# One-core hybrid attention block: value rows per head and partition, heads' outputs through DRAM, values one item behind, and a shorter start

## The chip, the core and the metric

One core of a Trainium2 chip runs the whole program. The metric is the device time of one execution in microseconds (us); the time before is the median of three runs. TensorE is called PE, VectorE DVE, ScalarE ACT, GpSimd POOL; SP issues most DMAs. "x" beside a row is a count, and a granted clock of 1.00 is PE's full clock.

## The reference, cut to what matters

A block on x of 1024 tokens by 1024 channels, in float32: an RMS norm, one wide projection, stick-breaking attention (8 heads of 64), an HGRN2 recurrence (4 heads of 128), a gated merge, and an MLP of width 4096.

```python
xn = rmsnorm(x, norm1_g[layer])
u = xn @ w_in[layer]
q_sb, k_sb, v_sb, f_raw, i_hg, q_hg, g_hg, gate_sb, gate_hg = split(u)
z = einsum('bhqd,bhkd->bhqk', qi, k) * scale
log_beta = log_sigmoid(z)
log_rem = where(mask, log_beta - z, 0)
between = cumsum(log_rem, axis=3, reverse=True) - log_rem
w = where(mask, exp(log_beta + between), 0)
o_sb = einsum('bhqk,bhkd->bhqd', w, v)
o_hg = hgrn2_chunkwise(silu(q_hg), k_hg, i_hg, log_f)   # then norm, * silu(g_hg)
merged = g_a * (o_sb @ w_o_sb) + g_b * (o_hg @ w_o_hg)
h = x + merged @ w_out
out = rmsnorm(h + square(relu(rmsnorm(h) @ w_ff1)) @ w_ff2)
```

## The kernel before

**Precision and product counts.** A float32 matrix is used as a high and a low part (a "split": ACT casts the high part at L154, DVE subtracts it at L159), so each product is three matmuls. `hi_lo_sent` makes the low part another way: ACT copies the negated value, and an accumulating DMA of POOL adds the source. Large products are done with seven instead of eight half-size products, which need sums of halves of the weights (`ValuePair`, blocks "11", "12", "21", "22") and of the normalised input (the forms of `early_form`, built from `early_whole`, which copies a high part and lets a POOL DMA add the low part).

**The start (0 to 186 us).** x is normalised and transposed in halves of 512 tokens (`norm_transpose`; its low parts xnl are DVE's, L346). In the gaps of that work the stream `front` runs the first head's q and k projection (`pjqk`) and the first two products of the values v and of HGRN's inputs i. `raw_units[0]` is the first block of attention's output gate: its product 1 (`pga`) and product 4 (`pgq`), which uses the weight wga0t, split from block 21 less a sum of other blocks. Finished values go to the DRAM table `vrows`, one row per token, 512 wide (8 heads x 64), behind a row of zeros.

**Attention (186 to 400 us).** 64 items (head h, block qb), in the order qb = 7, 0, 6, 1, 5, 2, 4, 3 within a head. An item's scores z (PE) give 1 - beta by a sigmoid (ACT, tile rm), a product scan on DVE (L1093) turns them into cumulated remainders, PE transposes these (`pw`), and ACT and DVE evict them as high and low weights wTh and wTl (L1141, L1147). Weights are used as differences, so V is the difference of neighbouring value rows: `v_load` reads the rows twice, once shifted by one, and `v_split` subtracts and splits them. Two items with neighbouring qb (7 and 6, 0 and 1, 5 and 4, 2 and 3) share a values product (`values`, tile po, numbered head_qc); it runs when the second item of the pair lies two items back. Scores run two items ahead and the scan one. Between them the loop takes steps of a fill stream (`st`): gate and HGRN projections `pga`, `pgq`, `pjf`, `pjq`. PE executes in order; main work and fill are two lanes, and a block of fill may not start before the main block two back.

A head's outputs ot have its own 64 rows twice, as a high and a low share; one half is written by an ACT DMA to rows of `osb` (SBUF, a pair of heads each), the other is added there by a POOL DMA.

**After attention (400 us on).** HGRN levels with raw jobs 5 to 7 of the gates as fill, the merge, and the MLP. Jobs 4 to 7 put `osb` 0 to 3 into the product with w_o_sb. In jobs 1 to 7, product 4 runs first and ACT copies it out of PSUM (p14); DVE adds the first half of product 1 to it.

Of the kernel before, what the change touches and what calls it, by code (L numbers as in the profile page):

```python
# [14 lines left out]
ALU = mybir.AluOpType  # L15
# [4 lines left out]
P = 128  # L20
# [19 lines left out]
def kernel(  # L40
# [34 lines left out]
    def slot(name, dt=F32):  # L75
        return spool.tile([P, 1024], dt, tag="s", name=name)
# [11 lines left out]
    def dram(name, shape):  # L88
        return scratch.tile(shape, F32, tag=name, name=name)
# [48 lines left out]
    def load(dst, src):  # L138
        last_load[0] = after(nc.sync.dma_start(dst, src), last_load[0])
# [38 lines left out]
    def halves():  # L178
        return ((i, slice(i * 512, (i + 1) * 512)) for i in range(2))
# [478 lines left out]

    qk, osb = {}, {}

    vrows = dram("vrows", [T + 1, SBW])
    vt, vraw = {}, {}

    def first_row():
        zero = half("vzero")[0:1, :]
        nc.gpsimd.memset(zero, 0.0)
        nc.gpsimd.dma_start(vrows[0:1, :], zero)

    def v_load(h):
        vraw[h] = slot(f"vr{h}")  # L670
        for i, cs in halves():
            load(
                vraw[h][:, cs].rearrange("p (t d) -> p t d", d=DHS),
                vrows[1 - i : T + 1 - i, h * DHS : (h + 1) * DHS].rearrange(
                    "(t p) d -> p t d", p=P
                ),
            )

    def v_split(h):
        r = vraw.pop(h)  # L680
# [61 lines left out]
    class ValuePair:  # L742
# [19 lines left out]
        def minus(self, out, x, y):  # L762
            for kp in range(2):
# [2 lines left out]
                    op=ALU.subtract,  # L766
                )

        WEIGHT = {1: "11", 2: "21", 3: "22", 4: "21", 5: "11", 6: "22", 7: "12"}

        def split(self, m):
# [39 lines left out]
        def p2(self, tb):  # L811
            v = half(f"v1{tb}")
            nc.scalar.copy(v, self.X[tb])
            Z = bank(f"viZ{tb}")
            yield from self.steps(2, {tb: Z}, True)
            nc.vector.tensor_tensor(out=v, in0=v, in1=Z, op=ALU.add)
            self.store(vrows, 1, 0, tb, v)

        def store(self, rows_, first, half_, tb, v):
            r0 = first + half_ * 512 + tb * P  # L820
            nc.gpsimd.dma_start(rows_[r0 : r0 + P, :], v)

        def x4(self):
            banks = {tb: bank(f"viP{tb}") for tb in range(4)}
# [13 lines left out]
        def x7(self):  # L838
            self.product(7, self.X, False)
            for tb in range(4):  # L840
                self.u3[tb] = half(f"vu3{tb}")
                nc.scalar.copy(self.u3[tb], self.X[tb])
                v = self.p4[tb]
                nc.vector.tensor_tensor(out=v, in0=v, in1=self.X[tb], op=ALU.add)
                self.store(vrows, 1, 1, tb, v)

        def y5(self):
            self.Y = {tb: bank(f"viY{tb}") for tb in range(4)}
            self.product(5, self.Y, True)
            for tb in range(4):  # L850
                v = self.u3[tb]
                self.last = add(v, v, self.Y[tb])
                self.store(irows, 0, 1, tb, v)

        def y3(self):
            self.product(3, self.Y, False)
            for tb in range(4):
                v = self.u2[tb]
                nc.vector.tensor_tensor(out=v, in0=v, in1=self.Y[tb], op=ALU.add)
                self.store(irows, 0, 0, tb, v)  # L860

    irows = dram("irows", [T, HGW])
    vi = ValuePair()
# [290 lines left out]
        return (h, qc) if seen[h, qc] == 2 else None  # L1154

    ots, sums = {}, deque()

    def values(h, qc):
        open_block("main")
        tiles = wTt.pop((h, qc))  # L1160
        nkb = 2 * qc + 2
        po = bank(f"po{h}_{qc}")[:, 0:256]
        for kb in range(nkb):
            for i in range(2):
                matmul(
                    po,
                    v_stat(h, kb),
                    tiles[kb // 4][i][:, kb % 4, :],
                    start=kb == 0 and i == 0,
                    stop=kb == nkb - 1 and i == 1,  # L1170
                )
        if qc in (3, 0) and h not in ots:
            ots[h] = [slot(f"ot{h}"), 0]
        ot = ots[h][0]
        nc.scalar.copy(ot[:, qc * 256 : (qc + 1) * 256], po)
        ots[h][1] += 1
        if ots[h][1] == 4:
            pair, r = h // 2, (h % 2) * DHS
            if pair not in osb:
                osb[pair] = slot(f"osb{pair}")  # L1180
            dst, other = osb[pair][r : r + DHS, :], ot[DHS - r : 2 * DHS - r, :]
            nc.scalar.dma_start(dst, ot[r : r + DHS, :])
            sums.append(lambda: nc.gpsimd.dma_start(dst, other, accum_op=ALU.add))

# [49 lines left out]
    def hg_job(h, key):  # L1234
        c0, ep = {
            "f": (C_F, f_epilogue), "q": (C_QH, lambda h: silu_epilogue(h, "q")),
            "g": (C_GH, lambda h: silu_epilogue(h, "g")),
        }[key]
        u = cols_unit(f"w{key}{h}", [(W_IN, c0 + h * P, P)])
        u.sent = h == 0  # L1240
        j_hg[h] = proj_jobs([(f"pj{key}{h}", u, ep(h))], xn)

    def hg_jobs(h):
# [328 lines left out]
    def raw_job(cb):  # L1572
        u = raw_units[cb]

        def steps_of(ps, wt, w0, half_, k0, start):
            wh, wl = u.hl[wt]
            for k in range(4):
                c = (w0 + k) * P
                xh, xl = xn.mov(k0 + k, half_)
                three(  # L1580
                    ps, wh[:, c : c + P], wl[:, c : c + P], xh, xl, start and k == 0, k == 3, True
                )
                if k % 2 == 1:
                    yield

        def body():
            p1, p14, g1 = (half(f"{n}_{cb}") for n in ("p1", "p14", "g1"))
            if cb >= 6:
                load_g1(cb - 6)
            if cb:  # L1590
                p4 = bank(f"pgq{cb}")
                yield from steps_of(p4, 1, 0, 1, 4, True)
                nc.scalar.copy(p14, p4)
            ps = bank(f"pga{cb}")
            yield from steps_of(ps, 0, 0, 0, 0, True)
            hi_behind[0] = nc.scalar.copy(p1, ps)
            nc.scalar.dma_start(pd[cb][:, 0, :], p1)
            if cb:
                st.prefetch()
            hi_behind[0] = None  # L1600
            if cb:
                add(p14, p1, p14)
            else:
                p4 = bank(f"pgq{cb}")
                yield from steps_of(p4, 1, 0, 1, 4, True)
                add(p14, p1, p4)
            nc.gpsimd.dma_start(pd[cb][:, 1, :], p14)
            yield from steps_of(ps, 0, 4, 0, 4, False)
            nc.scalar.activation(g1, ps, AF.Sigmoid, bias=gate_bias(0, cb))
            nc.scalar.dma_start(gd[cb], g1)  # L1610
            if cb >= 4:
                a_sb.put(cb - 4, osb[cb - 4])

        return st.add([u], body)

# [809 lines left out]
    norm1(range(4, NT))  # L2425
    front.advance(10, 1)
    raw_units[0].split()
    norm_transpose(xn, 1, 0, 4, None, lambda: front.advance(1, 1))
    turns["on"] = False
    for kp in range(2):  # L2430
        for b in ("12", "22"):
            vi.load(b, kp)
    turn_vectors(1, 6)
    lower_bounds()
    first_row()
    vi.minus("11", "12", "11")
    for half_, j in ((1, 0), (1, 1), (0, 0)):
        early_whole(half_, j)
    front.finish(j_first)
    raw_units[0].split_t()  # L2440
    vi.minus("12", "22", "12")
    vi.minus("22", "22", "11")
    vi.minus("21", "21", "22")
    vi.split(4)
    st.finish(j_raw[0])
    blocks = [qk_parts(h) for h in range(1, NHS)] + [(((C_GH, P),), g_store)]
    proj = [ProjPair(i, *blocks[2 * i : 2 * i + 2]) for i in range(4)]
    proj[0].load()
    early_op((1, 1), (1, 0), (1, 1), ALU.add)
    early_op((1, 0), (0, 0), (1, 0), ALU.subtract)  # L2450
    vi.x4()
    early_op((0, 0), (1, 1), (0, 0), ALU.subtract)
    early_form(6, *early_at((0, 0)))
    vi.split(6)
    early_form(7, *early_at((1, 0)))
# [58 lines left out]
    for i, it in enumerate(items):  # L2514
        if i + 1 < len(items):
            weights(*items[i + 1])
        if i + 2 < len(items):
            scores(*items[i + 2])
        if i % 2 == 1:
            next(wsums, None)  # L2520
        ahead = it[0] + 1
        if ahead < NHS and i % NHS in (1, 2, 6):
            {1: v_load, 2: qk_load, 6: v_split}[i % NHS](ahead)
        if sums and i % NHS == 4:
            sums.popleft()()
        want = n_first + (i + 1) * (n_fill - n_first) // len(items)
        st.advance(want - done, j_first_hg)
        done = want
        before = ready.popleft()[1] if ready and ready[0][0] < i - 1 else None

        def between():
            if before:
                values(*before)

        r = turn(*it, between)
        if i == len(items) - 2:
            attended[0] = turn_lo[0]
        if it[1] != NT - 1:
            between()
        if r:  # L2540
            ready.append((i, r))
# [141 lines left out]
```

## Time and profile before

| | |
|---|---|
| three runs | 1466.84, 1470.25, 1471.27 us |
| median | 1470.25 us |
| the profiled execution | 1469.17 us, span 1467.5 us |
| mean granted clock of PE | 0.994 |
| DMA moved over the span | 280.21 MB, mean 191 GB/s |

All durations come from the one profiled execution. Its span runs from the first to the last instruction; 1.7 us of its time lie around it. Busy PE at a clock below 1.00 is PE doing the same work longer, so idle time alone does not tell PE's whole loss.

### The profile page before, as it was taken

Reading aid. Unit: us, or ns where it says so; the run is one execution under the profiler, and the core shown is the slowest. Engines: PE = TensorE matmul, PEld = TensorE weight load, DVE = VectorE, ACT = ScalarE, POOL = GpSimd, SP = SyncE. Lnnn points to the kernel's source line nnn. Section 1 sums busy time; section 2 is a strip of 40 time slices with the busy share of each in tenths; the row PEclk is TensorE's granted clock in tenths of the full one; section 3 lists DMA queues with packets and bytes.
Section 4 is the critical chain, followed back from the end, with each engine's and each line's share of the span. In section 5 each row is a group of like instructions: output and inputs, shape, how many; then the busy total and the mean of one; then the engine's idle time right before and its main releaser. Section 6 shows DMA issues by size and latency. Waiting matters only on the chain. (4 is left out here: it accounts for less than half of the span.)

```text
span 1467.5 us, 19123 instructions
## 1 busy us (share of the span) xinstructions
PE 1422.1 (97%) x6990; PEld 1185.8 (81%) x6990; DVE 1069.0 (73%) x1486; ACT 683.3 (47%) x1115; POOL 183.0 (12%) x343
## 2 busy tenths in 40 slices
PE   8899999997999999999999999999999999999997
PEld 7678877786788888888887788888888888888886
DVE  6856568886976868668876898666776766768765
ACT  6553457665634434333334575444444533533433
POOL 3231222323100001101011110000000000000032
PEclk9999999999999999999999999999999999999999
DMA  9786699999512326855359623444444975676824
GB/s 307 167 279 186 194 256 235 216 214 204 118 58 65 101 65 206 289 170 174 130 184 300 212 93 129 158 158 158 158 158 158 348 267 201 232 277 244 281 104 181
DMA packets 187430, 280.21 MB, mean 191 GB/s; under 512 B 44444, under 2 KB 108488, under 8 KB 187336
## 3 DMA queue, kind: packets, MB, share of 16 engines
q1 hardware_dynamic: 163256, 207.41, 43.9%
q0 software_dynamic: 19696, 62.93, 15.5%
q10 hardware_dynamic: 4384, 8.65, 1.8%
q8 instruction: 55, 0.90, 0.3%
q14 instruction: 39, 0.32, 0.1%
HBM read 191.39 MB, written 83.36 MB: 187 GB/s over the span
## 5 line engine op out<-in xcount | busy, mean ns | idle before, releaser
L1093 DVE TENSOR_TENSOR_SCAN rm<-rm,bits 128x512 f32<-128x512 f32 (+6 forms) x72 | 87.5, 1223 | 23.9 <-ACT rm L1067 23.8
L154 ACT CAST whid<-w 128x1024 fp32r<-128x1024 f32 x30 | 31.6, 1053 | 153.3 <-PE pm L131 85.4
L131 PE MATMUL pm<-wlod,sh 128*128 128x512 f32 x240 | 93.5, 390 | 0.0
L131 PE MATMUL pm<-whid,sl 128*128 128x512 f32 x240 | 93.4, 389 | 0.0
L131 PE MATMUL pm<-whid,sh 128*128 128x512 f32 x240 | 93.4, 389 | 0.0
L131 PE MATMUL pm<-tl,sh 128*128 128x512 f32 (+1 forms) x210 | 81.3, 387 | 0.0
L131 PE MATMUL pm<-th,sl 128*128 128x512 f32 (+1 forms) x210 | 81.3, 387 | 0.0
L131 PE MATMUL pm<-th,sh 128*128 128x512 f32 (+1 forms) x210 | 81.3, 387 | 0.0
L159 DVE TENSOR_TENSOR wlod<-w,whid 128x1024 fp32r<-128x1024 f32 x30 | 36.7, 1223 | 56.2 <-ACT whid L154 56.1
L2239 POOL TENSOR_SCALAR fss<-fss 128x1 f32<-128x1 f32 x8 | 4.5, 562 | 562.5 <-ACT fsc L2234 561.9
L159 DVE TENSOR_TENSOR sl<-sa,sh 128x1024 fp32r<-128x1024 f32 x56 | 68.3, 1219 | 1.2 <-ACT sh L154 1.2
L1141 ACT ACTIVATE wTh<-pw,minus_one 128x128 fp32r<-128x128 f32 (+3 forms) x96 | 55.2, 597 | 29.3 <-PE pw L134 24.4
L154 ACT CAST sh<-sa 128x1024 fp32r<-128x1024 f32 x56 | 57.2, 1046 | 7.2 <-DMA sa<-ad 7.2
L1067 ACT ACTIVATE rm<-z 128x512 f32<-128x512 f32 (+3 forms) x96 | 44.4, 503 | 28.0 <-PE z L131 20.8
L1147 DVE SCALAR_TENSOR_TENSOR wTl<-pw,wTh 128x128 fp32r<-128x128 f32 (+3 forms) x96 | 49.7, 544 | 10.0 <-ACT wTh L1141 6.5
L131 PEld LDWEIGHTS pm<-wlod,sh 128*128 128x128 f32 x240 | 45.0, 188 | 9.8 <-DVE wlod L159 0.6
L131 PEld LDWEIGHTS pm<-whid,sh 128*128 128x128 f32 x240 | 45.1, 188 | 9.4
L131 PEld LDWEIGHTS pm<-whid,sl 128*128 128x128 f32 x240 | 45.0, 187 | 9.4
L134 PE MATMUL pw<-ident,rm 128*128 128x128 f32 x288 | 44.5, 279 | 6.8 <-DVE rm L1093 6.6
L131 PE MATMUL pX<-sql,t1h 128*128 128x512 f32 x128 | 50.0, 391 | 0.4 <-DVE sql L159 0.4
L131 PE MATMUL pX<-sqh,t1l 128*128 128x512 f32 x128 | 50.0, 390 | 0.1
L131 PE MATMUL pX<-sqh,t1h 128*128 128x512 f32 x128 | 49.8, 389 | 0.0
(986 smaller groups left out, 4451.9 us busy)
## 6 DMA issues: line engine op xcount, KB each, us to landing
w<-in_w_ff_dram SPq DMA_DIRECT2D x72, 512.0 KB, 4.8
sa<-ad SPq DMA_DIRECT2D x56, 512.0 KB, 6.7
ad<-a SPq DMA_DIRECT2D x32, 256.0 KB, 4.3
ad<-s SPq DMA_DIRECT2D x16, 512.0 KB, 3.8
tw<-in_w_out_dram POOLq DMA_DIRECT2D x24, 256.0 KB, 8.9
vi<-in_w_in_dram SPq DMA_DIRECT2D x10, 512.0 KB, 4.8
x<-in_x_dram SPq DMA_DIRECT2D x8, 512.0 KB, 7.6
qkh<-qkh POOLq DMA_DIRECT2D x16, 256.0 KB, 4.1
```

Source lines behind the costliest of these rows:

```text
L131: return pe(nc.tensor.matmul(*a, **k))
L134: return pe(nc.tensor.transpose(dst, src, ident))
L154: hi_last[0] = after(in_turn("act", nc.scalar.copy(dst, src)), hi_behind[0])
L159: nc.vector.tensor_tensor(out=dst, in0=src, in1=hi.bitcast(F32), op=ALU.subtract),
L1067: nc.scalar.activation(rm[:, s0 : s0 + m], z[:, :m], AF.Sigmoid, scale=-0.125)
L1093: sc = nc.vector.tensor_tensor_scan(out=rr, data0=rr, data1=bits[:, 1024 - nk + a : 1024 - nk + b][:, ::-1], initial=rm[:, b : b + 1] if i ...
L1141: nc.scalar.activation(th[:, 0:n, qs], src, AF.Identity, bias=minus_one),
L1147: nc.vector.scalar_tensor_tensor(out=tl[:, 0:n, qs], in0=src, scalar=-1.0, in1=th[:, 0:n, qs].bitcast(F32), op0=ALU.add, op1=ALU.subtract,),
L2239: nc.gpsimd.tensor_scalar(out=ssq, in0=ssq, scalar1=1.0 / D, scalar2=EPS, op0=ALU.mult, op1=ALU.add)
```

## The change

What it does, part by part:

1. `vrows` is laid out per head and partition: head h, partition p, then 64 values of each of the 8 token tiles, behind a tile that holds zero in its last partition. A store of v now writes pieces of 64 values; a load of a head's rows is 128x512, 127x512 and 1x512 in rows of 2 KB.
2. `v_split` of the next head moves from item 6 to item 5 of a head; `values` runs when its second item lies one item back.
3. `osb` in SBUF becomes a DRAM table `osd`, to which ACT's and POOL's DMAs write; raw jobs 5, 6 and 7 load it back (one pair, one pair, two pairs).
4. In jobs 5 to 7 product 4 runs after the first half of product 1 and is added straight from PSUM, as in job 0.
5. The first HGRN head's weights no longer use `hi_lo_sent`.
6. In the start, blocks "12" and "22" are loaded and "11" and "21" formed before the second half's transposes; wga0t follows these; "21" is made without the changed "22", as (21 - 22) + (12 - 11). `vi.split(4)` and one `early_op` move too.

```diff
-    vrows = dram("vrows", [T + 1, SBW])
+    vrows = dram("vrows", [NHS, P, (NT + 1) * DHS])
...
     def v_load(h):
-        vraw[h] = slot(f"vr{h}")
-        for i, cs in halves():
-            load(
-                vraw[h][:, cs].rearrange("p (t d) -> p t d", d=DHS),
-                vrows[1 - i : T + 1 - i, h * DHS : (h + 1) * DHS].rearrange(
-                    "(t p) d -> p t d", p=P
-                ),
-            )
+        r = vraw[h] = slot(f"vr{h}")
+        n = NT * DHS
+        load(r[:, :n], vrows[h, :, DHS:])
+        load(r[1:P, n:], vrows[h, 0 : P - 1, DHS:])
+        load(r[0:1, n:], vrows[h, P - 1 : P, :n])
...
+        def plus(self, out, x, y):
+            for kp in range(2):
+                add(self.raw[out, kp], self.raw[x, kp], self.raw[y, kp])
...
+            t = half_ * 4 + tb
+            if rows_ is vrows:
+                dst = rows_[:, :, (t + 1) * DHS : (t + 2) * DHS].rearrange("h p d -> p h d")
+                v = v.rearrange("p (h d) -> p h d", d=DHS)
...
+    osd = [dram(f"osd{pair}", [P, T]) for pair in range(NHS // 2)]
...
-            if pair not in osb:
-                osb[pair] = slot(f"osb{pair}")
-            dst, other = osb[pair][r : r + DHS, :], ot[DHS - r : 2 * DHS - r, :]
+            dst, other = osd[pair][r : r + DHS, :], ot[DHS - r : 2 * DHS - r, :]
...
-        u.sent = h == 0
...
-            if cb:
+            outs = {5: (0,), 6: (1,), 7: (2, 3)}.get(cb, ())
+            for pair in outs:
+                osb[pair] = slot(f"osr{pair}")
+                load(osb[pair], osd[pair])
+            alone = 0 < cb < 5
+            if alone:
                 p4 = bank(f"pgq{cb}")
                 yield from steps_of(p4, 1, 0, 1, 4, True)
                 nc.scalar.copy(p14, p4)
...
-            if cb:
+            if alone:
                 add(p14, p1, p14)
...
-            if cb >= 4:
-                a_sb.put(cb - 4, osb[cb - 4])
+            for pair in outs:
+                a_sb.put(pair, osb[pair])
...
-    norm_transpose(xn, 1, 0, 4, None, lambda: front.advance(1, 1))
-    turns["on"] = False
     for kp in range(2):
         for b in ("12", "22"):
             vi.load(b, kp)
+    vi.minus("11", "12", "11")
+    early_whole(0, 0)
+    norm_transpose(xn, 1, 0, 4, None, lambda: front.advance(1, 1))
+    turns["on"] = False
+    raw_units[0].split_t()
+    vi.minus("21", "21", "22")
+    vi.plus("21", "21", "11")
     turn_vectors(1, 6)
     lower_bounds()
     first_row()
-    vi.minus("11", "12", "11")
-    for half_, j in ((1, 0), (1, 1), (0, 0)):
-        early_whole(half_, j)
+    early_whole(1, 0)
+    early_whole(1, 1)
     front.finish(j_first)
-    raw_units[0].split_t()
+    vi.split(4)
     vi.minus("12", "22", "12")
     vi.minus("22", "22", "11")
-    vi.minus("21", "21", "22")
-    vi.split(4)
...
-        if ahead < NHS and i % NHS in (1, 2, 6):
-            {1: v_load, 2: qk_load, 6: v_split}[i % NHS](ahead)
+        if ahead < NHS and i % NHS in (1, 2, 5):
+            {1: v_load, 2: qk_load, 5: v_split}[i % NHS](ahead)
...
-        before = ready.popleft()[1] if ready and ready[0][0] < i - 1 else None
+        before = ready.popleft()[1] if ready else None
```

What this does to the engines' order. First DVE in the start, from the sum for wga0r on (vi110 and so on are the sums of blocks, v10 to v13 finished values, xnl1 the low parts of the second half). Before:

```order
L1497 TENSOR_TENSOR wga0r1_213<-wga0r0_211,wga0r1_213 128x1024
L816 TENSOR_TENSOR v10_504<-v10_504,viZ0_506 128x512
L1497 TENSOR_TENSOR wga0r1_213<-wga0r1_213 128x512
L346 SCALAR_TENSOR_TENSOR xnl10_526<-xnt10_0_527,prm_93,xnh10_525 128x512
L346 SCALAR_TENSOR_TENSOR xnl10_526<-xnt11_0_545,prm_93,xnh10_525 128x512
L816 TENSOR_TENSOR v11_534<-v11_534,viZ1_536 128x512
L346 SCALAR_TENSOR_TENSOR xnl11_559<-xnt12_0_560,prm_93,xnh11_558 128x512
L346 SCALAR_TENSOR_TENSOR xnl11_559<-xnt13_0_578,prm_93,xnh11_558 128x512
```

And now:

```order
L1504 TENSOR_TENSOR wga0r1_217<-wga0r0_215,wga0r1_217 128x1024
L764 TENSOR_TENSOR vi110_195<-vi120_529,vi110_195 128x1024
L1504 TENSOR_TENSOR wga0r1_217<-wga0r1_217 128x512
L764 TENSOR_TENSOR vi111_199<-vi121_533,vi111_199 128x1024
L820 TENSOR_TENSOR v10_508<-v10_508,viZ0_510 128x512
L346 SCALAR_TENSOR_TENSOR xnl10_546<-xnt10_0_547,prm_93,xnh10_545 128x512
L346 SCALAR_TENSOR_TENSOR xnl10_546<-xnt11_0_565,prm_93,xnh10_545 128x512
L820 TENSOR_TENSOR v11_554<-v11_554,viZ1_556 128x512
L346 SCALAR_TENSOR_TENSOR xnl11_579<-xnt12_0_580,prm_93,xnh11_578 128x512
L764 TENSOR_TENSOR vi210_203<-vi210_203,vi220_531 128x1024
L346 SCALAR_TENSOR_TENSOR xnl11_579<-xnt13_0_598,prm_93,xnh11_578 128x512
```

Two sums stand ahead of v10, and vi210, vi211 and one plus among the xnl that follow; the operation that makes wga0t stands directly behind the last xnl, where it stood behind the projection's last low part and seven sums.

Second, PE at the end of head 3 and the start of head 4 (pw3_4 are the transposes of head 3's block 4, z4_0 the scores of head 4's block 0, po3_2 the values of head 3's blocks 4 and 5; its first two of twelve matmuls are shown). Before:

```order
L134 MATMUL pw3_4_1_2867<-ident_75,rm3_4_2764 128x128
L131 MATMUL z4_0_0_2874<-KS4_2710,QH4_2708 128x256
L131 MATMUL z4_0_0_2874<-KS4_2710,QL4_2709 128x256
L134 MATMUL pw3_3_0_2883<-ident_75,rm3_3_2810 128x128 x4
L131 MATMUL z4_6_0_2892<-KS4_2710,QH4_2708 128x512
L131 MATMUL z4_6_0_2892<-KS4_2710,QL4_2709 128x512
L131 MATMUL z4_6_512_2896<-KS4_2710,QH4_2708 128x384
L131 MATMUL z4_6_512_2896<-KS4_2710,QL4_2709 128x384
L134 MATMUL pw4_7_1_2904<-ident_75,rm4_7_2839 128x128 x4
L131 MATMUL po3_2_2911<-wTh3_2_0_2774,V3_2577 128x256
L131 MATMUL po3_2_2911<-wTl3_2_0_2775,V3_2577 128x256
```

And now:

```order
L134 MATMUL pw3_4_1_2875<-ident_75,rm3_4_2791 128x128
L131 MATMUL z4_0_0_2882<-KS4_2718,QH4_2716 128x256
L131 MATMUL z4_0_0_2882<-KS4_2718,QL4_2717 128x256
L134 MATMUL pw3_3_0_2891<-ident_75,rm3_3_2824 128x128 x4
L131 MATMUL po3_2_2898<-wTh3_2_0_2801,V3_2565 128x256
L131 MATMUL po3_2_2898<-wTl3_2_0_2802,V3_2565 128x256
```

The values stand ahead of z4_6 and of the next head's first transposes. In the same way po_3 of a head moves from behind pw_5 to directly behind pw_1.

Third, SP's queue where the loads for head 4 are issued (vr4 are its value rows, KS, QH and QL its keys and queries). Before:

```order
L139 DMA vr4_2669<-vrows_98 128x8x64 x2
L139 DMA KS4_2710<-qkh4_107 64x1024
L139 DMA QH4_2708<-qkh4_107 64x1024
L139 DMA KS4_2710<-qkl4_108 64x1024
L139 DMA QH4_2708<-qkh4_107 64x1024
L139 DMA QL4_2709<-qkl4_108 64x1024 x2
```

And now:

```order
L139 DMA vr4_2688<-vrows_98 128x512
L139 DMA vr4_2688<-vrows_98 127x512
L139 DMA vr4_2688<-vrows_98 1x512
L139 DMA KS4_2718<-qkh4_107 64x1024
L139 DMA QH4_2716<-qkh4_107 64x1024
L139 DMA KS4_2718<-qkl4_108 64x1024
```

The order is the same; the two value loads in pieces of 64 values are three in rows of 512.

More of the change, by code (lines that the diff above doesn't have):

```diff
@@ L666, in first_row @@
         nc.gpsimd.memset(zero, 0.0)
-        nc.gpsimd.dma_start(vrows[0:1, :], zero)
+        nc.gpsimd.dma_start(
+            vrows[:, P - 1 : P, 0:DHS].rearrange("h p d -> p h d"),
+            zero.rearrange("p (h d) -> p h d", d=DHS),
+        )
     def v_load(h):
-        vraw[h] = slot(f"vr{h}")
-        for i, cs in halves():
-            load(
-                vraw[h][:, cs].rearrange("p (t d) -> p t d", d=DHS),
-                vrows[1 - i : T + 1 - i, h * DHS : (h + 1) * DHS].rearrange(
-                    "(t p) d -> p t d", p=P
-                ),
-            )
+        r = vraw[h] = slot(f"vr{h}")
[3 more added lines that the diff above has]
+        load(r[0:1, n:], vrows[h, P - 1 : P, :n])
     def v_split(h):
@@ L816, in p2, with store @@
             nc.vector.tensor_tensor(out=v, in0=v, in1=Z, op=ALU.add)
[L817 to L821, printed above, removed]
+            self.store(vrows, 0, tb, v)
+        def store(self, rows_, half_, tb, v):
+            t = half_ * 4 + tb
+            if rows_ is vrows:
+                dst = rows_[:, :, (t + 1) * DHS : (t + 2) * DHS].rearrange("h p d -> p h d")
+                v = v.rearrange("p (h d) -> p h d", d=DHS)
+            else:
+                dst = rows_[t * P : (t + 1) * P, :]
+            nc.gpsimd.dma_start(dst, v)
         def x4(self):
@@ L844, in x7 @@
                 nc.vector.tensor_tensor(out=v, in0=v, in1=self.X[tb], op=ALU.add)
-                self.store(vrows, 1, 1, tb, v)
+                self.store(vrows, 1, tb, v)
         def y5(self):
@@ L852, in y5 @@
                 self.last = add(v, v, self.Y[tb])
-                self.store(irows, 0, 1, tb, v)
+                self.store(irows, 1, tb, v)
         def y3(self):
@@ L859, in y3 @@
                 nc.vector.tensor_tensor(out=v, in0=v, in1=self.Y[tb], op=ALU.add)
-                self.store(irows, 0, 0, tb, v)
+                self.store(irows, 0, tb, v)
     irows = dram("irows", [T, HGW])
@@ L2450 @@
     early_op((1, 0), (0, 0), (1, 0), ALU.subtract)
+    early_op((0, 0), (1, 1), (0, 0), ALU.subtract)
     vi.x4()
-    early_op((0, 0), (1, 1), (0, 0), ALU.subtract)
     early_form(6, *early_at((0, 0)))
```

## The prediction

> **What bounds the kernel now.** I read the page first, then busy time by stage, then the waits of TensorE (PE), then the granted clock behind each long wait, and last the queues in the stage that loses most.
>
> ```profile
> span 1467.5 us, 19123 instructions
> PE 1422.1 (97%) x6990; PEld 1185.8 (81%) x6990; DVE 1069.0 (73%) x1486; ACT 683.3 (47%) x1115; POOL 183.0 (12%) x343
> ```
>
> PE is busy for 1422.1 of 1467.5 us. The change leaves PE's matmuls as they are and only moves them, so all it can win is the 45.4 us in which PE idles, and time in which PE runs at a lower clock. By stage (start, attention, the rest, the last tiles):
>
> ```profile
> 0.00:186.00 186.00, 176.26 (x812) 145.60 (x813) 122.71 (x161) 91.28 (x135) 52.21 (x99) 0.98 0.75 226
> 186.00:400.00 214.00, 191.72 (x1139) 163.98 (x1137) 169.58 (x241) 137.68 (x286) 57.87 (x130) 0.98 0.91 206
> 400.00:1440.00 1040.00, 1034.31 (x4951) 860.07 (x4950) 762.83 (x1066) 444.95 (x681) 68.51 (x106) 1.00 0.54 183
> 1440.00:1467.50 27.50, 19.84 (x92) 16.16 (x91) 13.85 (x20) 9.44 (x16) 4.39 (x8) 0.95 0.33 122
> ```
>
> The first two figures of a row after the window are its length and PE's busy time: 9.7 us idle in the start, 22.3 in attention, 5.7 in 1040 us behind it. In attention DMA is at 0.91 and DVE at 170 of 214 us, so little is spare there. PE's waits, by what ended them:
>
> ```profile
> PE pw L134 <- DVE rm L1093: 6.6, 8, 1.8
> PE z L131 <- DMA QL<-qkl: 5.3, 3, 3.0
> PE z L131 <- DMA QH<-qkh: 4.0, 2, 3.2
> PE pgq L131 <- DVE wga0t L159: 2.9, 1, 2.9
> ...
> PE pjf L131 <- DMA wf0l<-wf0r: 2.2, 1, 2.2
> ...
> PE pga L131 <- ACT p L1596: 1.4, 2, 0.7
> PE po L131 <- DVE wTl L1147: 1.3, 3, 0.5
> ...
> PE po L131 <- ACT wTh L1141: 0.5, 1, 0.5
> ...
> PE pgq L131 <- ACT wga0t L154: 0.5, 1, 0.5
> PE pjq L131 <- DMA wq0l<-wq0r: 0.5, 1, 0.5
> ```
>
> Each row is total us, times, longest. A wait also costs clock behind it (the figure ahead of the DMA share is the granted clock):
>
> ```profile
> 60.00:65.00 5.00, 5.00 (x13) 3.83 (x13) 4.82 (x6) 1.05 (x1) 0.00 (x0) 0.50 1.05 224
> 260.00:265.00 5.00, 5.00 (x27) 4.59 (x27) 1.08 (x3) 0.47 (x1) 3.07 (x5) 0.66 0.69 196
> 340.00:345.00 5.00, 5.00 (x26) 4.43 (x25) 4.26 (x6) 4.06 (x10) 0.00 (x0) 0.81 0.86 134
> 360.00:365.00 5.00, 2.03 (x11) 1.37 (x10) 4.06 (x5) 2.43 (x7) 4.14 (x12) 1.00 0.79 168
> ```
>
> PE is full in the first three. They lose 5 x 0.50 = 2.5 us behind the wga0t wait, 5 x 0.34 = 1.7 behind wf0l and 5 x 0.19 = 1.0 behind QH. The fourth holds a QL wait of 3.0 us and stays at 1.00, so a wait of 2 to 3 us costs clock only sometimes.
>
> **The change part by part.** *The start.* Product 4's gate weight wga0t is late because DVE takes seven sums first:
>
> ```profile
> 36.80 0.68 DVE L816 TENSOR_TENSOR v<-v,viZ 128x512 f32<-128x512 f32 x1
> ...
> 47.16 1.40 DVE L346 SCALAR_TENSOR_TENSOR xnl<-xnt,prm,xnh 128x512 fp32r<-128x512 f32 x2
> ...
> 49.87 8.40 DVE L764 TENSOR_TENSOR vi<-vi,vi 128x1024 f32<-128x1024 f32 x7
> ...
> 58.79 0.68 DVE L159 TENSOR_TENSOR wga0t<-wga0r,wga0t 128x512 fp32r<-128x512 f32 x1
> ```
>
> After the change wga0t stands right behind the last xnl, so 2.9 + 0.5 of wait and 2.5 of clock go: -5.9. The price is that four sums and the new plus (five operations of 128x1024, 8.40 / 7 = 1.2 each) now stand ahead of that xnl. From 36.80 on DVE has 5 x 1.2 + 4 x 0.6 (three v, the half of wga0r) + 8 x 0.7 (xnl) = 14.0 without a gap: the last xnl ends at about 50.8 where it ended at 48.56. PE's projection of q and k for the first head waits for it: +2.2; I take **+2.0**, since PE could be late for another reason at that point. Sum **-3.9** (bounds -5.9 and 0, the latter if the xnl's PSUM banks, held until v is added, stop PE's transposes as well).
>
> *Two weights without POOL.* wf0 and wq0 of the first HGRN head lose the accumulating DMA; DVE makes their low parts instead, 2 x 1.2 us more in 214 us where it is busy for 170. The waits go: 2.2 + 0.5, and 1.7 of clock: **-4.4** (bounds -2.2, if a slow DVE takes its place, and -4.9).
>
> *Value rows and what SP queues behind them.*
>
> ```profile
> 315.37 5.00 SPq L139 DMA_DIRECT2D vr<-vrows  x2
> 320.47 4.63 SPq L139 DMA_DIRECT2D KS<-qkh  x1
> ...
> 326.45 0.55 SPq L139 DMA_DIRECT2D KS<-qkl  x1
> vr<-vrows SPq DMA_DIRECT2D x16, 256.0 KB, 9.6
> SPq L139 <- DMA osb<-ot: 25.0, 3, 10.1
> ```
>
> In the timeline of SP's queue a head's two value loads (1024 pieces of 256 bytes each) take 5.00 us to issue, and the first load of the next head's q and k behind them takes 4.63, where its like takes 0.55 later on. After the change there are three loads in pieces of 2 KB, an eighth as many pieces. So I expect some 1.5 us for the values and 0.5 for KS, and QH and QL more than 6 us earlier, against waits of at most 3.2. The QL wait of 3.0 stands behind osb's stores (last row), whose pieces now go to DRAM, and need not go wholly. Of 9.3 us of waits and 1.0 of clock I take **-8.5** (bounds -5 and -10.3). The loads of 256-byte pieces took 9.6 us to land (fourth row; us to landing is its last figure). The Trainium skill, page "DMA: Bandwidth & Descriptors", section "Specifications", gives 512 bytes as the least transfer for line rate, with a read-modify-write below. By it these loads reach full rate and all 10.3 go, 1.8 more than I take; and it speaks against the change in the stores, which are cut into the 256-byte pieces now.
>
> ```profile
> L821 POOL DMA_DIRECT2D vrows<-vp x4: 542/544/547, 103.5 to 105.3; - x4
> ...
> L1219 POOL DMA_DIRECT2D v<-irows x4: 967/974/1233, 382.1 to 535.2; - x4
> ```
>
> POOL issues a plain row store in 0.54 us and a load in 1024 pieces in 0.97 (min/median/max in ns): eight stores cost POOL 0.43 each. The last four leave at 105, some 65 us before the first value load, so they are covered. Three of the first four now stand ahead of four of the transfers from which DVE forms the sums for x6: 1.3 us later. I put that at zero, since PE waits for none of them now; without cover it is the second rival.
>
> *V cast an item earlier, values one item behind.* Here PE loses. At the end of head 3:
>
> ```profile
> 291.24 0.60 PE L134 MATMUL pw<-ident,rm 128*128 128x128 f32 x4
> ...
> 294.75 0.39 PE L131 MATMUL po<-wTl,V 128*128 128x256 f32 x1 [0.41 <-DVE wTl L1147]
> ...
> 292.29 1.23 DVE L1093 TENSOR_TENSOR_SCAN rm<-rm,bits 128x512 f32<-128x512 f32 x1 [0.43 <-ACT rm L1067]
> 293.43 0.67 DVE L159 TENSOR_TENSOR V<-vr,V 128x512 fp32r<-128x512 f32 x1
> 294.01 0.88 DVE L1147 SCALAR_TENSOR_TENSOR wTl<-pw,wTh 128x512 fp32r<-128x512 f32 x2
> ```
>
> The transposes pw3_3 end near 291.8; now po3_2 follows at once, where z4_6 and pw4_7 stood between. It needs the low weights wTl of pw3_4, which DVE can begin at 293.5, behind the scan (V's low part is gone from between), and whose first ends at 294.1: a wait of **2.3**. Behind it on PE wait z4_6, and so the sigmoids and the scan of the next item but one, which cost nothing more while that scan has an item's time in hand. Six of the seven boundaries where the order changes (all but the last head's) have a piece of fill between pw and po:
>
> ```profile
> 288.63 0.39 PE L131 MATMUL pjf<-xnh,wf0h 128*128 128x512 f32 x1
> ...
> 289.99 0.62 PE L131 MATMUL z<-KS,QL 128*128 128x512 f32 x2
> ```
>
> Six matmuls, 289.99 - 288.63 = 1.4 us. So po_2 costs 2.3 + 6 x (2.3 - 1.4) = 7.7. Qc 3's values, po_3, now follow pw_1 directly:
>
> ```profile
> 281.90 0.38 PE L134 MATMUL pw<-ident,rm 128*128 128x128 f32 x2
> ...
> 282.32 1.13 DVE L1147 SCALAR_TENSOR_TENSOR wTl<-pw,wTh 128x512 fp32r<-128x512 f32 x2
> ```
>
> pw_1 is through at 282.2 and the first of two wTl (1.13 / 2 each) at 282.9: 0.7 a head, 5.6 for eight. po_0 I put at 1, being small, and 1.5 stays of the old scan waits: 15.8 in all. That replaces 6.6 + 1.3 + 0.5 = 8.4, so **+7** (bounds 0, if the moved wait only stands where the scan's stood and all 7.4 vanish, and +16 if nothing of the old goes).
>
> *The heads' outputs through DRAM, and product 4 in jobs 5 to 7.* Four loads of 512 KB join SP's queue and eight stores change their end; that stage has DMA at 0.54 and PE idle for 5.7 us in 1040. If such a load waits for its slot or for the sum, the loads of gate weights queue behind it on SP, and PE needs these jobs later. Cost zero; were that cover gone, about the 9.6 us of landing for one of them. Job 5 to 7 take product 4 straight from PSUM, and the waits pga <- p go: -1.4. Against it two pairs of outputs are cast in job 7, the last with PE close behind: one cast of 1.2. Together **0** (bounds -1.4 and +2).
>
> The sum: -3.9 - 4.4 - 8.5 + 7 + 0 = -9.8. The profiled execution took 1469.17 us, 1.7 more than its span and 1.1 less than the median of 1470.25; 1469.2 - 9.8 = 1459.4, so I say **1460**.
>
> **The rivals.** *Values cost nothing.* If DVE, with V's parts out of the way, has the weights when PE arrives, the term is 0 and the DMA term full: -3.9 - 4.9 - 10.3 = -19.1, **1450**. For it: 0.7 us of lateness per head is within what a fill moves. Against: the 2.3 us at head 3 stand behind a scan that the change leaves.
>
> *No change: the gains are eaten.* Either SP's queue is slow for the load of the DMA engines (0.91) and not for the pieces, and QH and QL stay: -9.8 + 8.5 = -1.3; or the start's sums and stores hold PE up, so that -3.9 becomes 0, and the values cost 5 more: -0.9. Both give about **1468**. For the first: the share of 0.91. Against: the KS load behind the values is slow and the one 6 us later is not.
>
> *Slower.* The boundary's wait stays at 2.3 us at all seven heads, because the fill goes where DVE and ACT work on its epilogue too, and each costs clock as wf0l's 2.2 did, 1.7: 6 x 1.4 + 7 x 1.7 = 20 more, -9.8 + 20 = +10, **1479**. It decides from waits above about 2 us. For it: the row at 260. Against: the row at 360, and that ACT and DVE worked through fills before. The Trainium skill, page "TensorE: Matmul & The Clock Gate", section "Part 1: The HAM clock gate", lets the clock fall after one idle window of about 3.4 us, free-running. By it waits of 2.3 us cost no clock, and this rival comes to 1468; the trace, with 0.66 behind a wait of 2.2 us, does not bear out the length.
>
> **How the numbers follow.** Forecast 0.45 (its own range 1454 to 1466), values free 0.17 (1446 to 1454), no change 0.23 (1466 to 1474), slower 0.15 (1475 to 1485). The range leaves out the slower case and little of the lowest: 1447 to 1474. A measurement here tells 0.3%, 4.4 us, from no change; the bounds are 1465.8 and 1474.7. Faster takes the forecast and the first rival: 0.62; within 0.3% the third: 0.23; slower 0.15.
>
> **What would show it.** Right: the rows of PE for wga0t, wf0l, wq0l, QH and QL are gone or under 3 us together, and the clock from 60 to 65 is 1.00; SP issues KS behind the values in about 0.5 us; PE's waits for wTl and wTh grow from 1.8 us to above 10, while pw <- rm shrinks below 3. Wrong: KS still takes above 3 us; po's waits below 5 (the first rival) or above 20 with a clock below 0.97 in attention (the slower one); or the projection pjqk waits above 3 us for xnl.

## The result and the profile after

| | before | after |
|---|---|---|
| median | 1469.03 us (4 runs) | 1510.74 us (1508.32 to 1512.81, 4 runs) |
| ratio | | 1.0283 (95% interval 1.0259 to 1.0307) |
| span of the profiled execution | 1467.5 us | 1506.6 us |

The change made the kernel 41.7 us slower. The forecast was 1460 us, 10 us faster, and its slowest rival stood at 1479. The page of the changed kernel:

```profile
span 1506.6 us, 19099 instructions
PE 1436.0 (95%) x6990; PEld 1196.3 (79%) x6990; DVE 1072.5 (71%) x1490; ACT 680.8 (45%) x1110; POOL 181.0 (12%) x341
```

PE's matmuls are as many as before. PE is busy 14 us longer for them, because its mean clock fell from 0.994 to 0.982, and idle 25 us longer. Busy time by stage (window, length, then PE's busy time; the figure ahead of the DMA share is the granted clock):

```profile
0.00:186.00 186.00, 176.71 (x821) 146.57 (x822) 121.28 (x159) 90.87 (x134) 54.82 (x98) 0.99 0.76 227
186.00:440.00 254.00, 205.52 (x1127) 172.42 (x1126) 174.96 (x246) 135.83 (x282) 56.31 (x129) 0.91 0.69 169
440.00:1479.00 1039.00, 1034.33 (x4955) 861.15 (x4955) 763.52 (x1068) 445.63 (x681) 65.55 (x106) 1.00 0.54 186
1479.00:1506.60 27.60, 19.43 (x92) 16.15 (x90) 12.77 (x20) 8.46 (x15) 4.37 (x8) 0.93 0.30 111
```

All of it is in attention: 48.5 us idle where it had 22.3, and a clock of 0.91 where it had 0.98. The DMA engines did not get busier: their share there fell from 0.91 to 0.69. PE's waits in the whole run, the largest and those that the prediction names:

```profile
PE pga L131 <- DVE wTl L1156: 10.6, 2, 6.0
PE po L131 <- DVE wTl L1156: 9.5, 8, 4.2
PE z L131 <- DMA QL<-qkl: 8.4, 4, 3.7
PE z L131 <- DMA QH<-qkh: 6.6, 3, 2.3
...
PE po L131 <- ACT wTh L1150: 2.6, 4, 1.0
PE pjqk L131 <- DVE xnl L346: 2.6, 2, 1.3
...
PE xnt L134 <- DVE v L820: 1.8, 1, 1.8
```

wga0t, wf0l and wq0l are gone as forecast, but QL and QH wait longer (15.0 for 9.3), and DVE's weights wTl are waited for 20 us. DVE's own waits in attention tell why; first the changed kernel's row, then that of before:

```profile
DVE vr L681 <- DMA vr<-vrows: 32.1, 5, 10.3
```

```profile
DVE vr L681 <- DMA vr<-vrows: 3.0, 1, 3.0
```

DVE stands 32 us in all for the heads' value rows. One of these waits in the timelines of the changed kernel, SP's queue, DVE and PE:

```profile
227.84 14.95 SPq L139 DMA_DIRECT2D vr<-vrows  x3
242.90 0.45 SPq L139 DMA_DIRECT2D KS<-qkh  x1
...
255.57 0.69 DVE L681 TENSOR_TENSOR vr<-vr 128x512 f32<-128x512 f32 x1 [9.66 <-DMA vr<-vrows]
256.18 0.42 DVE L1156 SCALAR_TENSOR_TENSOR wTl<-pw,wTh 128x256 fp32r<-128x256 f32 x1
...
256.66 0.80 PE L131 MATMUL pga<-xnh,wga2whi 128*128 128x512 f32 x1 [5.96 <-DVE wTl L1156]
```

The three value loads hold SP's queue for 15 us, and the rows that DVE waits for are there 12.8 us after that (255.6 - 242.8). The subtraction of value rows at L681 sits in DVE's order ahead of wTl, wTl frees a PSUM bank that the fill's pga needs, so PE stands 6 us and runs slowly behind it (0.43 us between matmuls at 258, 0.23 in a warm stretch).

### The profile page after: what moved, and what is told of

It is laid out like the page before. It is cut to its first block, busy times and chain, and to the rows that moved or that the text cites. A ratio compares the mean times of both kernels' runs of the same rounds, so it can differ in the third digit from the quotient of the medians.

```text
span 1506.6 us, 19099 instructions
## 1 busy us (share of the span) xinstructions
PE 1436.0 (95%) x6990; PEld 1196.3 (79%) x6990; DVE 1072.5 (71%) x1490; ACT 680.8 (45%) x1110; POOL 181.0 (12%) x341
## 5 line engine op out<-in xcount | busy, mean ns | idle before, releaser
L131 PE MATMUL po<-wTh,V 128*128 128x256 f32 x160 | 44.2, 307 | 6.8 <-DVE wTl L1156 4.2
```

The lines of the kernel that those rows point to most:

```text
L131: return pe(nc.tensor.matmul(*a, **k))
```

## The experiments

All runs are of one core. "Before" was run beside each group: 1467.5, 1467.9, 1468.3 and 1469.1 us.

| run | median us | ratio to before (95% interval) |
|---|---|---|
| e1_split_load | 1479.54 | 1.0070 (1.0043 to 1.0096) |
| e2_old_rows | 1472.66 | 1.0029 (1.0012 to 1.0046) |
| e3_rows_alone | 1526.19 | 1.0395 (1.0362 to 1.0428) |
| e4_rows_split_alone | 1465.88 | 0.9981 (0.9967 to 0.9996) |
| e5_values_two_behind | 1456.90 | 0.9910 (0.9885 to 0.9935) |
| e6_values_two_behind_v5 | 1453.84 | 0.9898 (0.9879 to 0.9918) |
| e7_sent | 1473.58 | 1.0039 (1.0024 to 1.0054) |
| e8_split_two_behind | 1461.55 | 0.9948 (0.9929 to 0.9968) |
| e9_padded_two_loads | 1455.08 | 0.9915 (0.9896 to 0.9934) |
| e10_outputs_alone | 1460.37 | 0.9954 (0.9940 to 0.9969) |
| e11_v5_sent | 1458.34 | 0.9937 (0.9920 to 0.9953) |
| e12_split_113_14 | 1501.79 | 1.0231 (1.0205 to 1.0257) |
| e13_outputs_slots_held | 1461.50 | 0.9947 (0.9930 to 0.9965) |
| e14_po3_one_behind | 1464.84 | 0.9965 (0.9952 to 0.9979) |
| e15_po2_one_behind | 1454.03 | 0.9904 (0.9883 to 0.9926) |

### Which load, and why it is slow

```diff
-        load(r[1:P, n:], vrows[h, 0 : P - 1, DHS:])
+        load(r[1:113, n:], vrows[h, 0:112, DHS:])
+        load(r[113:P, n:], vrows[h, 112 : P - 1, DHS:])
```

> The changed kernel, but the load of 127 rows is cut into one of 112 and one of 15 rows. Theory S (the load of 127 rows goes out over too few DMA engines, lands 10 us and more late, and DVE, PE and SP's queue stand behind it): the value loads issue in under 3 us together, DVE's 32.1 us of waiting for vr fall below 5, the time falls by 35 to 55 us to 1455 to 1475. Rival R1 (V is needed an item earlier and values follow one item behind, so DVE and PE wait whatever the load does): the waits on vr shrink little, time above 1495. Rival R2 (the 256-byte stores and the new table are what is slow): time above 1495 as well, with PE losing in the start and DMA share higher.

31.2 us went with one load cut in two, and DVE's waits for vr dropped out of its list. R1 and R2 miss this time by more than 15 us. S is closest, but the time is 4.5 us above its range, and the value loads still take 1.6 to 6.7 us to issue where it expected under 3. e2 has the table and loads of before:

> The changed kernel with the value table of before: rows of 512 per token, two loads of a head in 256-byte pieces. All else is changed as before. S: DVE's waits for vr fall below 8 us, the time comes to 1460 to 1480, above the split load by what the two 256-byte loads hold up in SP's queue (some 4 to 10 us). R1: above 1495. R2: 1455 to 1475, no slower than the split load.

Another 6.9 us below. The time is in S's range, but S put this run above the split load and it lies below; R2's number for this run fits as well, and only e1 speaks against R2. Now the new table in the kernel of before, whole and with the cut:

> The kernel of before with the new value table and its three loads alone; V is cast at item 6 and values follow two items behind, as before. S: most of the loss is here without any other part: 1490 to 1515, and the loads issue in 7 to 15 us. R1: no loss, 1460 to 1475. R2: 1490 or more.

> The kernel of before with the new value table, its load of 127 rows cut into 112 and 15. S: 1455 to 1466, that is the QH and QL waits of 9.3 us mostly gone, nothing lost. R1: the same. R2: 1490 or more.

Without any other part the table costs 58.7 us (1526.2 for 1467.5); with the cut it gives 1.7. The loss is larger than S expected, and the small gain of e4 isn't the one that S named: PE still waits 11.9 us for QL and QH there. In e3 DVE's waits:

```profile
DVE vr L681 <- DMA vr<-vrows: 57.4, 7, 20.9
```

The cut at 113 asks whether it is the number 127 or the length of one load:

```diff
-        load(r[1:113, n:], vrows[h, 0:112, DHS:])
+        load(r[1:114, n:], vrows[h, 0:113, DHS:])
```

> As the split load, but cut into 113 and 14 rows in place of 112 and 15. If the number of engines follows from what divides the number of rows (113, as 127, has no divisor but 1): as slow as the whole load, 1495 to 1515, with DVE waiting over 20 us for vr. If only the cut into two loads helped: as 112 and 15, 1476 to 1483.

One row more, and 22.3 us are back (1501.8 for 1479.5), as forecast for the case that the number of rows decides. DVE's waits in e12:

```profile
DVE vr L682 <- DMA vr<-vrows: 23.1, 7, 8.4
```

So neither the two loads nor the bytes decide, but the number of rows in one load. The Trainium skill, page "DMA: Bandwidth & Descriptors", section "Why a DMA increments its semaphore by 16 and not by 1", states it: a DMA goes out over the largest number of engines, up to 16, that divides the slowest dimension of both sides, and it names 127 partitions as a case with one. e12 agrees (113 is slow, 112 is not). The traces don't name the engine of a packet, so the single engine itself is not shown. They do show how long the rows take: from the first to the last of a head's 256 packets of 2 KB it is 17 to 25 us in the changed kernel, 15 to 24 in e12 and 3 to 8 in e1.

### Whether 2 KB rows are worth anything

```diff
+    vrows = dram("vrows", [NHS, P + 1, NT * DHS])
...
+        load(r[:, :n], vrows[h, 1 : P + 1, :])
+        load(r[:, n:], vrows[h, 0:P, :])
```

> Values two items behind, V cast at item 5, and a value table with a leading row per head that repeats partition 127 one tile later, so that both value loads have 128 rows of 2 KB and no load of 127 rows is left; seven small stores are added in the start. Theory S with L (a load costs by its number of rows that share engines, and each further load in SP's queue waits for an earlier one): no QL waits, as fast as old rows with V at item 5 (1453.8) or up to 6 us faster, 1447 to 1455. Rival (rows of 2 KB cost as such, or the 256-byte stores do): 1458 to 1466, as with the load cut in two.

1455.1 against 1453.8 with the old rows (e6): no difference that these runs can tell, though all loads have 2 KB rows. So loads of 256-byte pieces cost nothing here that the times can tell. A further load seems to: e8 has the load cut in two (four loads a head), e5 the old rows (two loads); apart from the table, which by e9 costs nothing that the runs can tell, all else is the same.

> The changed kernel with the load of 127 rows cut into 112 and 15, values two items behind and V cast at item 6. V: 8 to 16 us below the split load alone (1479.5), 1464 to 1471; and not below the run with the old rows and values two behind by more than 3 us, since QL still waits. O: 1475 to 1482.

1461.6 against 1456.9, below the range of 1464 to 1471 but not as fast as the old rows, and e8's PE waits in attention have a row that e5's lack:

```profile
PE z L131 <- DMA QL<-qkl: 7.8, 4, 3.4
```

In e8's attention SP's queue stands 25.3 us for the gate's stores (gd<-g) and 21.5 for the outputs' (osd<-ot), in e5 5.1 and 12.3. Why two further loads lead to this, and whether it is what makes QL late, is not shown.

### Values one item behind

Values two items behind, with V cast at item 6 (e5) and at item 5 (e6), and the old rows in both:

```diff
-        before = ready.popleft()[1] if ready else None
+        before = ready.popleft()[1] if ready and ready[0][0] < i - 1 else None
```

> The changed kernel with the value table of before, and with values two items behind and V cast at item 6 as before (part 2 of the change undone; start, weights without POOL, outputs through DRAM and jobs 5 to 7 stay changed). Theory V (values one item behind is what costs in attention): against the kernel with the old rows alone undone (1472.7) PE's waits for wTl and wTh fall from 10.4 to below 4 us and the time by 8 to 14 us, to 1458 to 1465. Rival O (the outputs' DMAs through DRAM or the two weights made on DVE are what costs): no gain, 1469 to 1476.

> As the run before, but V is still cast at item 5. V: within 3 us of it, since V's two operations only move; a little faster if they were on the path from the scan to the weights. Rival: if the cast at item 5 is what costs, this one stays near 1472 and only the run before gains.

15.8 us go with part 2 undone (a little more than V's 8 to 14) and 18.8 with the values alone undone, so values one behind cost 16 to 19. The runs can't tell the two versions apart (the intervals of e5 and e6 overlap), so where V is cast is worth nothing that is shown. PE's waits in attention, e2 (one behind), then e6 (two behind):

```profile
PE po L131 <- DVE wTl L1151: 8.6, 12, 1.6
PE pw L134 <- DVE rm L1097: 5.7, 7, 1.7
PE pga L131 <- ACT p L1603: 3.0, 2, 1.8
PE po L131 <- ACT wTh L1145: 1.8, 2, 1.3
```

```profile
PE pw L134 <- DVE rm L1097: 5.6, 9, 1.2
...
PE po L131 <- DVE wTl L1151: 0.5, 1, 0.5
PE po L131 <- ACT wTh L1145: 0.5, 1, 0.5
```

po's waits are 10.4 for 1.0, and the scan's did not shrink. All rows of that view come to 21.5 and 13.0 us: 8.5 of waiting. The granted clock is the figure ahead of the DMA share, 0.96 and 1.00; rows of e2, e6 and, for later, e14 in this order:

```profile
186.00:400.00 214.00, 192.04 (x1109) 161.88 (x1108) 166.22 (x233) 130.01 (x274) 52.52 (x123) 0.96 0.84 195
```

```profile
186.00:400.00 214.00, 200.85 (x1205) 172.26 (x1204) 182.25 (x264) 137.51 (x286) 54.75 (x126) 1.00 0.87 206
```

```profile
186.00:400.00 214.00, 195.50 (x1148) 167.30 (x1147) 174.97 (x252) 134.89 (x282) 54.89 (x126) 0.98 0.87 203
```

214 x 0.04 = 8.6 us of clock and 8.5 of waits make 17.1 of the 18.8. The clock is not lost evenly. Cut into windows of 5 us, e2's attention has five with a clock from 0.63 to 0.69 and one at 0.97, and all the others are at 1.00; e6 has none below 1.00. The first of e2 (last row), with the window and the two waits ahead of it:

```profile
207.66 0.41 PE L134 MATMUL pw<-ident,rm 128*128 128x128 f32 x2 [1.71 <-DVE rm L1097]
...
209.80 0.39 PE L131 MATMUL po<-wTl,V 128*128 128x256 f32 x1 [1.62 <-DVE wTl L1151]
...
205.00:210.00 5.00, 1.68 (x12) 1.19 (x11) 3.38 (x5) 2.49 (x5) 1.58 (x5) 1.00 1.04 282
210.00:215.00 5.00, 5.00 (x25) 4.69 (x25) 1.99 (x4) 0.00 (x0) 1.00 (x4) 0.66 1.14 333
```

Two waits, the second of them po_3's, leave PE 1.7 us of work in 5, and the next 5 us run at 0.66. The scan's wait alone costs no clock at this place: it is 1.15 us in e6 and 1.64 in e15, both at 1.00 behind it. e14 and e15 move one of the four values alone:

```diff
+        before = ready.popleft()[1] if ready and ready[0][0] < i - (ready[0][1][1] != 3) else None
```

> Old rows, V cast at item 5, and only po_3 (blocks 7 and 6) one item behind, directly behind pw_1; the other three two behind. The forecast's share for po_3 is 5.6 us: 1457 to 1462 against 1453.8. If po_2 at the head's end carries the cost: within 3 us of 1453.8.

> Old rows, V cast at item 5, and only po_2 (blocks 5 and 4) one item behind, at the head's end behind pw_3. The forecast's share is 7.7 us less the scan waits that it replaces; if clock behind these waits is what was left out: 1459 to 1468, with a granted clock of 0.96 to 0.98 in attention. If po_3 carries the cost: within 3 us of 1453.8.

e14 is 11.0 us slower than e6 (1464.8 for 1453.8; 9.8 by the ratios to each group's own before) and above its forecast range, e15 0.2. Rows of e14, then of e15:

```profile
PE po L131 <- DVE wTl L1151: 6.0, 6, 1.6
```

```profile
PE po L131 <- DVE wTl L1151: 3.9, 8, 0.9
PE po L131 <- ACT wTh L1145: 2.2, 3, 1.0
```

po_3's waits grew by 5.5, the clock fell to 0.98. Not all of it is po_3's: e14's longest wait is for the gate weight wga4t (1.4 us in e6), and clock goes behind it:

```profile
325.75 0.77 PE L131 MATMUL pgq<-xnh,wga4t 128*128 128x512 f32 x2 [3.12 <-DMA wga4t<-wga4r]
...
325.00:330.00 5.00, 4.25 (x13) 3.38 (x14) 1.66 (x3) 0.48 (x1) 0.55 (x1) 0.66 0.97 272
```

That is 1.7 us of wait and 5 x 0.34 = 1.7 of clock. In e15 po_2 waits 5 us more too, never above 1.0, the scan's waits fall by 1.1, and the time grows by no more than the runs can tell. The remaining 7.6 us of 18.8 (18.8 - 11.0 - 0.2) belong to po_0, po_1 or the parts together; they were not tried apart. Two places in e2 that the prediction priced, po_3 in head 3 and po_2 at its end:

```profile
284.31 0.39 PE L131 MATMUL po<-wTl,V 128*128 128x256 f32 x1 [0.68 <-DVE wTl L1151]
```

```profile
296.38 0.58 PE L131 MATMUL po<-wTh,V 128*128 128x256 f32 x1 [1.32 <-ACT wTh L1145]
...
297.83 0.58 PE L131 MATMUL po<-wTl,V 128*128 128x256 f32 x1 [0.87 <-DVE wTl L1151]
```

0.7 and 1.32 + 0.87 = 2.2 us, as worked out (0.7 and 2.3). The second pair of matmuls takes 0.58 us each, the first 0.39: the clock is 0.63 from 295 to 300. So po_2's waits cost clock there, behind a scan wait of 0.85 at 293.6; in e15 waits of 1.04 and 0.88 at this place cost none.

### The other parts

The outputs through DRAM with jobs 5 to 7, alone in the kernel of before, and the same with the four SBUF slots held as before:

> The kernel of before with the outputs through DRAM and jobs 5 to 7 changed alone. If this part is what took the QH and QL waits away in the runs with old rows: those waits fall from 9.3 to below 3 us and the time is 1457 to 1464. If it was another part (the weights without POOL, the start): the waits stay above 6 us, 1464 to 1470.

> The kernel of before with the outputs through DRAM and jobs 5 to 7 changed, but the four SBUF slots are taken at each pair's first output, as before, and stay held until they are loaded. If the slots that come free are what gave 8 us (loads of q, k and v and weights start earlier): back to 1465 to 1470, with QH and QL waits above 5 us. If the route or jobs 5 to 7 are: 1458 to 1463, as with free slots.

Both gain (8.0 and 7.6 us), so the freed slots are not the cause. The QH and QL waits of 9.3 us are gone in e10; in e13 1.3 is left. PE's transposes pw span 176.8 us in e10's trace and 185.1 in that of before, so the gain is in attention, and jobs 5 to 7 lie behind it. SP's wait for the output stores, 25.0 us before, is in e10:

```profile
SPq L139 <- DMA osd<-ot: 12.2, 2, 6.9
```

But this row is no measure of QL and QH: in e2, whose outputs go through DRAM too, it is 38.9 us, and PE waits for neither. Why the route gains stays open, and so does the share of jobs 5 to 7, which no run has apart from it. The two weights by POOL's DMA again, with values one behind and with two:

```diff
+        u.sent = h == 0
```

> The changed kernel with the value table of before, and with the first HGRN head's two weights made by ACT and an accumulating DMA again. V and the prediction's own term: slower by 3 to 5 us, 1475 to 1478, with the waits for wf0l and wq0l back. Rival O: faster, below 1471, since DVE loses 2.4 us of work in attention.

> Old rows, values two items behind, V cast at item 5, and the first HGRN head's two weights by ACT and POOL's accumulating DMA as before. The prediction's term: slower by 3 to 5 us than without (1453.8), 1456 to 1460, with waits for wf0l near 2 us. Rival: no difference, 1451 to 1455.

1473.6 against 1472.7 tells nothing, where 3 to 5 us were forecast; 1458.3 against 1453.8 is 4.5 us. The size is the forecast's, the mechanism is not. In both runs PE does not wait for wf0l or wq0l at all, though POOL's DMA makes them. What e11 has more of than e6, where it is 1.4, is

```profile
PE pgq L131 <- DMA wga4t<-wga4r: 4.9, 1, 4.9
```

and e5, whose weights are made on DVE, waits 4.5 us there as well. So these runs don't show that the weights are what cost the 4.5 us.

## Why the prediction was wrong

| term | forecast | measured | from |
|---|---|---|---|
| load of 127 rows | not seen | +31.2 | after, e1 |
| two more loads per head | not seen | +6.9 | e1, e2 |
| values one behind and V at item 5 | +7 | +15.8 | e2, e5 |
| QH and QL by 2 KB rows | -8.5 | about 0 | e6, e9 |
| weights without POOL | -4.4 | -4.5 | e6, e11 |
| outputs and jobs 5 to 7 | 0 | -8.0 | before, e10 |
| start | -3.9 | +1.5 | the rest of e5 (its trace: about -1.8, item 5) |

The measured ones make 31.2 + 6.9 + 15.8 - 4.5 - 8.0 + 1.5 = 42.9, where 41.7 came. That is no test of the terms: they are differences along one chain of runs (after, e1, e2, e5, before), the start is what was left over, and the 1.2 us are what the kernel of before differs between groups. The first two rows belong together, too: the change has one load more per head than before, and e1 has two.

1. **The step that failed** is "So I expect some 1.5 us for the values and 0.5 for KS". It priced three loads by the number of their pieces, and its bound on the bad side, -5, let none of them be slower than the two before. KS does issue in 0.45 us, but the value loads take 7.5 to 15 us to issue and the rows 17 to 25 to move, because one load has 127 rows: that cost 31.2 us (e1). The row 127x512 stands in the order shown ahead of the prediction.
2. The QH and QL waits were put down to the value loads because these issue slowly ahead of KS. The runs say otherwise: 2 KB rows alone leave QL waits (11.0 us in e4, with four loads), old rows with the outputs through DRAM have next to none. SP's row for osb, 25.0 us, was shown, and used only for the part of the gain that might not come. The outputs, put at zero, gave 8.0 us, about what this term promised: that is luck, and not its mechanism.
3. Values: the sum of the waits came out near the forecast (8.5 us where 7 were), partly by luck: po's were put at 7.7 + 5.6 + 1 = 14.3 and came to 10.4, the scan's were to fall to 1.5 and stayed at 5.7. The clock was left out. It was put into the slower rival alone, from waits above 2 us; here it was lost with none above 1.8 in one piece in e2. The shares differ: 7.7 us were laid on po_2, which alone costs nothing that the runs can tell (e15), and 5.6 on po_3, which has 5.5 of waiting (e14), with up to 11.0 us of time, some 3.4 of it behind wga4t.
4. The weights without POOL: the size came out where values wait little (4.5 us), but not by the waits that the term was made of, which are absent with POOL's DMA too (e7, e11). That is luck as far as the traces tell. With values one behind, no gain shows.
5. The start: wga0t's wait went as forecast, but PE now waits 2.6 us for xnl where it waited 1.1, and 1.8 for v in the transposes, a price of 3.3 us for 2.0. The clock from 60 to 65 is 1.00 now, but 0.66 from 40 to 45. The value products end at 120.2 to 122.7 us in the twelve profiles with the new start and at 122.4 to 124.1 in the five with the old one: 1.8 us earlier on average, half of the forecast. The +1.5 by the rest of e5 is no more than these runs differ, so it doesn't speak against that. The start was not run alone.
6. The outputs cost 0 by the forecast, since they were judged in the stage where the loads are, and gave 8 us where the stores are.

Of the rivals none held. The slower one came to 1479 by 8.4 us of further waits and 11.9 of clock behind po_2's. e2 shows 8.6 us of such clock, but not behind po_2 alone (e15); the load of 127 rows was in none.

**A version that beats both** is e6, the change without its value table and with values two items behind: 1453.8 us, ratio 0.9898.

## What to carry to other kernels

Before a DMA is priced by bytes or pieces, look at how many rows it has: one load of 127 or 113 rows per head cost this kernel 22 to 60 us against one cut at 112. A few waits of 1 to 2 us in PE, full otherwise, can cost as much again in its clock (e2: 8.5 us and 8.6), and need not (e15); a forecast that counts waits alone may take half. A size that comes out right does not prove its mechanism: look whether the wait that was priced is there when the change is undone. A part that moves a transfer is to be judged where the transfer leaves as well as where it is read.

## What was not expected of the hardware

PE's granted clock fell to 0.96 over 214 us with no wait above 1.8 us. The Trainium skill, page "TensorE: Matmul & The Clock Gate", section "Part 1: The HAM clock gate", speaks of an idle window of about 3.4 us, and further down of another kernel whose clock swings because PE idles briefly and often. e2 agrees with the second: 0.66 behind waits of 1.71 and 1.62 us that follow each other. It gives no threshold, since 1.04 and 0.88 us cost nothing in e15. And loads in 256-byte pieces, 512 KB of them per head, ran as fast as loads in 2 KB rows as far as the kernel's time can tell (1453.8 and 1455.1 us).
